# Twenty-seven pairs of blocks by seven products, with their sums of weight blocks made ahead in the up stage

## The chip, the core and the metric

The kernel runs on one core of a Trainium2 chip. The metric is device time in microseconds (us), the median of repeated runs. One more execution is recorded by the hardware profiler; its page and trace are read below. The engines are TensorE (PE, with its weight loads as PEld), VectorE (DVE), ScalarE (ACT), GpSimd (POOL) and SyncE (SP), which here mostly issues DMA transfers.

## The reference, cut to what matters

One layer of an encoder block over 256 tokens of width 2048, float32 throughout:

```python
hn = rmsnorm(h, mix_norm_pre);  proj = hn @ w_in            # then an SSD mixer and a pooling mixer
h = h + rmsnorm(concat([y_ssd, y_pool]) @ w_out, mix_norm_post)
hn = rmsnorm(h, ffn_norm_pre);  up = hn @ w_up              # 2048 x 11264: gate and value halves
ff = (gelu(dwconv(gate)) * val) @ w_down                    # 5632 x 2048
h = h + rmsnorm(ff, ffn_norm_post)
gate = sigmoid(rmsnorm(h, ple_norm_pre) @ w_ple_gate)       # 2048 x 2048
h = h + rmsnorm(gate * (p @ w_ple), ple_norm_post)
```

Nearly all work is in the products with the weight matrices, about 200 MB of float32 that are read from DRAM once.

## The kernel before

**Precision.** Each operand of a product is split into a high part (a ScalarE copy that rounds, L150) and a low part (a VectorE subtraction, L151). A product is three matmuls: high by high, high by low, low by high, all issued at L87 (`mm`).

**Stages.** In order: the input projections (`dtu`, `xb`, `z` in the trace, with the mixers among them), the output projection (`wo`), a small product (`ple`), **up** (`ga` for the gate half, `va` for the value half: 88 units of one 1 MB load and 32 matmuls each), **down** (`dn`), a second small product, and **gate** (`gt`). Down and gate each go through their output columns in two halves of 1024. A half of down is 22 pairs of 128-row blocks of the weight (u = 0 to 21), a half of gate is 8 pairs.

**A pair.** In `token_major` a regular pair loads 1 MB (two row blocks by 1024 columns) into one of three `raw` buffers, splits it into two of five `whi`/`wlo` buffers, and runs 24 matmuls of 128x512. The activations (`hs`) are split at L865 for each pair in down. In a *fast* pair the 2x2 blocks (two token blocks, two row blocks, two column blocks) are multiplied by seven products in place of eight, Winograd's form of Strassen's scheme: 21 matmuls (`seven_products`). It needs sums of the weight's four blocks, made by three VectorE additions in the raw buffer (L250 over 128x1024, L251 and L252 over 128x512), and sums of the activations' blocks (`pair_sums`, L753 to L758: four subtractions or additions over 128x128, and a split over 128x512). Its results gather in four more PSUM banks (`alt`; `dns`, `dn0s`, `dn1s`, `gts` in the trace), which `combine` adds into the main ones (L262 to L276) after the unit that follows the last fast pair of a half.

Fast pairs before: in `wo` u = 5 and u = 2, 4; in down `(2, 5, 8, 11, 14, 17)` and `(2, 5, 8, 11, 14, 17, 19)`; in gate u = 4 and u = 2. For the four row pairs that come first in down, `hid_sums` keeps the activations' sums in two pages (`hsum`), so that the second half has them ready.

**Memory.** There are 13 pages of 1 MB (128 x 2048 floats). During up and down, two hold h (the residual), six the hidden activations (`hid`), and others the normalised input, the `ple` product and what a stage gathers.

**Order.** The program is written as one stream; the Tile scheduler keeps that order on each engine, and adds semaphores. Loads of weights stand in order on SP's queue, so one that waits for a buffer holds up those behind it. Jobs in the list `work` are run by `aside()`, one entry after each unit. In the second half of down, before u = 16, `first_gate` loads the gate's first pair (`gtf`, 1 MB) into a page and splits it there: a ScalarE pass at L905, a second read of the weight with an accumulating GpSimd DMA, and a ScalarE copy at L907. At the end of down the residual is updated (L807) and transposed and split (`dnx`, L189) for the gate.

In the gate's second half the order of row blocks is permuted (`ks`), and pages that have come free (`spare`) take the parts of some pairs.

Of the kernel before, what the change touches and what calls it, by code (L numbers as in the profile page):

```python
# [11 lines left out]
F32 = mybir.dt.float32  # L12
F32R = mybir.dt.float32r
AF = mybir.ActivationFunctionType
ALU = mybir.AluOpType

P = 128
L = 256
D = 2048
NK = D // P  # L20
DSSD = 1024
H = 16
DFF = 5632
# [28 lines left out]
def build(nc, a, out):  # L52
    x = a["x"][0]
    w_in, w_out, w_up = a["w_in"][0], a["w_out"][0], a["w_ffn_up"][0]
    w_down, w_gate, w_ple = a["w_ffn_down"][0], a["w_ple_gate"][0], a["w_ple"][0]
    out = out[0]

    with tile.TileContext(nc) as tc, \
# [12 lines left out]
        def page(name, dtype=F32):  # L71
            return gp.tile([P, 2048], dtype, tag="pg", bufs=13, name=name)

        def mid(name, dtype=F32):
            return gp.tile([P, 1024], dtype, tag="mid", bufs=3, name=name)
# [38 lines left out]
        last, sums_ = {}, {}  # L114

        def load(dst, src, ahead=False):

            with tc.issue_after(last["dma"]) if last and not ahead else nullcontext():
                return ins(nc.sync.dma_start(dst, src))
# [72 lines left out]
        work = []  # L192
# [10 lines left out]
                yield o, c  # L203
                c += o.shape[-1]

        def block_sums(name, w, which):


            jobs = []

            def step(c0, k, i):
                t = sums_[name, c0, k]
                v = t.rearrange("p (b c) -> p b c", b=4)
                if i == 0:
                    nc.gpsimd.dma_start(t.rearrange("p (k c) -> p k c", k=2),
                                        w[k * P:(k + 2) * P, c0:c0 + 1024].rearrange("(k p) c -> p k c", p=P))
                elif i == 1:
                    nc.gpsimd.dma_start(v[:, 0:2], w[k * P:(k + 2) * P, c0 + 512:c0 + 1024]
                                        .rearrange("(k p) c -> p k c", p=P), accum_op=ALU.add)
                elif i == 2:  # L220
                    nc.gpsimd.dma_start(v[:, 3], v[:, 0], accum_op=ALU.add)
                else:
                    nc.gpsimd.dma_start(v[:, 2], v[:, 3], accum_op=ALU.add)

            for c0, k in which:
                sums_[name, c0, k] = dp.tile([P, 2048], F32, tag=f"{name}s{c0}_{k}", bufs=1, name=f"{name}s{c0}_{k}")
            for j in range(len(which) + 3):
                jobs.append([lambda a_=(*which[j - i], i): step(*a_) for i in (3, 2, 1, 0) if 0 <= j - i < len(which)])
            return jobs

        def seven_products(name, stage, w, k0, c0, a_, acc, alt, start, stop):

            if (stage, c0, k0) in sums_:
                r = raw(f"{name}r", None, 0, 0)
                last["dma"] = load(r[:, 512:1536], w[(k0 + 1) * P:(k0 + 2) * P, c0:c0 + 1024], True)
                last["dma"] = load(r[:, :512], w[k0 * P:(k0 + 1) * P, c0:c0 + 512], True)
                t = page(f"{name}t")
                last["dma"] = load(t, sums_[stage, c0, k0], True)  # L240
                b11 = split(f"{name}a", r[:, :512], 512)
                b2 = split(f"{name}b", r[:, 512:1536], 1024)
            else:
                r = t = raw(f"{name}r", w[k0 * P:(k0 + 2) * P, c0:c0 + 1024]
                            .rearrange("(k p) c -> p k c", p=P), 2, 1024)
                b11 = split(f"{name}a", r[:, :512], 512)
                b2 = split(f"{name}b", r[:, 1024:], 1024)
                v = r.rearrange("p (b c) -> p b c", b=4)

                nc.vector.tensor_add(v[:, 0:2], v[:, 0:2], v[:, 1::2])  # L250
                nc.vector.tensor_add(v[:, 3], v[:, 3], v[:, 0])  # L251
                nc.vector.tensor_add(v[:, 2], v[:, 2], v[:, 3])  # L252
            t13 = split(f"{name}c", t[:, :1024], 1024)
            t42 = split(f"{name}d", t[:, 1024:], 1024)
            for x, (wh, wl), c, o, own in (
                    ("a11", b11, 0, alt[0], True), ("a12", b2, 0, acc[0][0], False), ("s4", b2, 512, acc[0][1], False),
                    ("s1", t13, 0, alt[1], True), ("s3", t13, 512, alt[2], True), ("a22", t42, 0, acc[1][0], False),
                    ("s2", t42, 512, alt[3], True)):
                xh, xl = a_[x]
                for q, (xx, ww) in enumerate(((xh, wh), (xh, wl), (xl, wh))):  # L260
                    mm(o, xx, ww[:, c:c + 512], own and start and q == 0, own and stop and q == 2)
# [175 lines left out]
        for u in range(0, NK, 2):  # L437
            r = [wp.tile([P, 2048], F32, tag="raw", bufs=3, name=f"dtur{u}") if u else r0, page(f"dtur{u + 1}")]
            for j in range(2):
                k = u + j  # L440
# [17 lines left out]
            for j in range(2):  # L458
                k = u + j
# [373 lines left out]
        pl = [ple(0)]  # L833
        rf = row_rstd("rf", h)
        rfb = along_tokens("rfb", rf)
        hid = [page(f"hid{i}") for i in range(6)]
        for s in range(DFF // 512):
            sc = mid(f"gr{s}")
            for i in range(2):
                ga = main(f"ga{s}{i}")  # L840
                feature_pairs(f"ug{s}{i}", w_up, s * 512 + i * 256, hf, ga)
                o = sc[:, i * 512:(i + 1) * 512]
                total(o, ga)
                v = o.rearrange("p (f t) -> p f t", f=2)
                nc.vector.tensor_tensor(v, v, rfb.unsqueeze(1).to_broadcast([P, 2, L]), op=ALU.mult)
            cv = conv(f"fc{s}", sc, 3, V_FCW + 4 * s, NF, V_FCB + 4 * s)
            nc.scalar.activation(cv, cv, AF.Gelu_apprx_tanh)  # L847
            nc.gpsimd.tensor_tensor(cv.rearrange("p (f t) -> p f t", f=4), cv.rearrange("p (f t) -> p f t", f=4),  # L848
                                    rfb.unsqueeze(1).to_broadcast([P, 4, L]), op=ALU.mult)
            for i in range(2):  # L850
                va = main(f"va{s}{i}")
                feature_pairs(f"uv{s}{i}", w_up, DFF + s * 512 + i * 256, hf, va)
                c0 = (s % 2) * 1024 + i * 512
                hd = hid[s // 2][:, c0:c0 + 512]
                total(hd, va)
                nc.vector.tensor_mul(hd, hd, cv[:, i * 512:(i + 1) * 512])
# [3 lines left out]
        def get_hid(k):  # L860
            if k % 2 == 0:
                t = lp.tile([P, 1024], F32R, tag="hs", bufs=2, name=f"hs{k}")
                src = hid[k // 8][:, (k % 8) * L:(k % 8 + 2) * L]
                nc.scalar.copy(t[:, :512], src)
                nc.vector.tensor_sub(t[:, 512:], src, t[:, :512].bitcast(F32))  # L865
                cur["t"] = t
            o = (k % 2) * L
            return cur["t"][:, o:o + L], cur["t"][:, 512 + o:512 + o + L]
# [7 lines left out]
                hcache[k0], hcache[k0 + 1] = get_hid(k0), get_hid(k0 + 1)  # L876
            return hcache[k]

        keep, kept = [], {}

        def hid_sums(k):


            (h1, l1), (h2, l2) = get_hid(k), get_hid(k + 1)
            if k not in kept:
                src = hid[k // 8][:, (k % 8) * L:(k % 8 + 2) * L]
                a11, a21, a12, a22 = (src[:, i * P:(i + 1) * P] for i in range(4))
                n = len(kept)
                if n in (0, 2):
                    keep.append(page(f"hsum{k}", F32R))  # L890
                o = keep[-1][:, n % 2 * 1024:(n % 2 + 1) * 1024] if n < 4 else mid(f"he{k}", F32R)
                d = pair_sums(f"hd{k}", mid(f"hd{k}"), o, a11, a21, a12, a22)
                if n < 4:
                    kept[k] = d
            else:
                d = dict(kept[k])
            d.update(a11=(h1[:, :P], l1[:, :P]), a12=(h2[:, :P], l2[:, :P]), a22=(h2[:, P:], l2[:, P:]))
            return d

        def first_gate():  # L900

# [6 lines left out]
            for j in range(2):  # L908
                ready[f"gt00_{j}"] = hi[:, j * 1024:(j + 1) * 1024], lo[:, j * 1024:(j + 1) * 1024]

        hp = sublayer("dn", w_down, list(range(NF)), hid_get, gload("gffn", a["ffn_norm_post"][0]), h, V_PN,
                      fast=((2, 5, 8, 11, 14, 17), (2, 5, 8, 11, 14, 17, 19)), sums=hid_sums, at={16: first_gate})


        pl.append(ple(1))
# [33 lines left out]
        for half in range(2):  # L949
# [1 line left out]
            alt = [] if half else main(f"gts{half}")  # L951
            acc = [main(f"gt{half}{t}") for t in range(2)]
            alt += main(f"gts{half}") if half else []
            ks, fast = list(range(NK)), (4,)
            if half == 1:
                ks, fast = [0, 1, 2, 3, 8, 9, 4, 5, 6, 7, 10, 11, 12, 13, 14, 15], (2,)

                for i in (8, 10):
                    sh, sl = page(f"gth{i}", F32R), page(f"gtl{i}", F32R)
                    for j in range(2):  # L960
                        spare[f"gt1{ks[i]}_{j}"] = (sh[:, j * 1024:(j + 1) * 1024], sl[:, j * 1024:(j + 1) * 1024])
# [68 lines left out]
```

## Time and profile before

| what | before |
|---|---|
| median of 3 runs | 1143.8 us (1143.8 to 1144.74) |
| the profiled execution | 1143.09 us, of which the span is 1141.3 |
| granted TensorE clock | 0.997 |
| instructions in the span | 15449 |
| PE busy | 1122.0 us |
| DVE busy | 868.8 us |
| ACT busy | 611.0 us |
| DMA, mean over the span | 193 GB/s |
| read from and written to DRAM | 216.99 MB and 2.10 MB |
| stages: up, down, small product and gate | about 303–798, 798–1036, 1036–1132 us |

Times inside the trace count from the start of the span. "Busy" is the time in which an engine executes; the chain of waits is the path that ended last, followed back step by step. `x` with a number counts instructions.

### The profile page before, as it was taken

How to read it: one execution, taken by the hardware profiler on the slowest of the kernel's cores; microseconds unless marked ns; L12 is line 12 of the kernel's file. 1: busy time of each engine (PE TensorE's matmuls, PEld its weight loads, DVE VectorE, ACT ScalarE, POOL GpSimd, SP SyncE). 2: the span in 40 equal slices, each digit the busy share in tenths (PEclk: the TensorE clock that was granted, in tenths of full speed). 3: DMA queues.
4: the chain of work that ended last, by engine and by line, in shares of the span. 5: the costliest groups of instructions: out<-in, count | busy, mean ns of one | idle time of the engine just before them, and what ended most of it. 6: DMA issues, size and time to landing. Idle time of an engine off the chain costs nothing.

```text
span 1141.3 us, 15449 instructions
## 1 busy us (share of the span) xinstructions
PE 1122.0 (98%) x6018; PEld 966.0 (85%) x6018; DVE 868.8 (76%) x1140; ACT 611.0 (54%) x830; POOL 124.9 (11%) x124
## 2 busy tenths in 40 slices
PE   9998999999999999999999999999999999999996
PEld 9997987888888888888888888888888888778885
DVE  6579896699876666666766756668888888789895
ACT  6633543565674554444544544545555565656562
POOL 0274504200110000000000000000000000001001
PEclk9999999999999999999999999999999999999999
DMA  9952347555556555555555565556566656666552
GB/s 358 341 184 75 111 151 267 200 160 190 172 190 205 196 190 185 184 185 186 189 191 193 181 204 186 185 184 222 157 212 221 200 170 220 194 221 205 181 196 74
DMA packets 129866, 220.09 MB, mean 193 GB/s; under 512 B 3713, under 2 KB 96769, under 8 KB 128897
## 3 DMA queue, kind: packets, MB, share of 16 engines
q1 hardware_dynamic: 129232, 217.70, 57.4%
q0 software_dynamic: 272, 1.05, 0.5%
q8 instruction: 47, 0.77, 0.3%
q10 hardware_dynamic: 288, 0.36, 0.1%
q14 instruction: 27, 0.21, 0.1%
HBM read 216.99 MB, written 2.10 MB: 192 GB/s over the span
## 4 chain that ended last, share of the span: by engine, by line
PE 90%; DVE 6%; ACT 1%; DMA 1%; issue 1%; POOL 1%; DVEq 0%; POOLq 0%; ACTq 0%
PE va L87 22%; PE ga L87 21%; PE dna L87 15%; PE gt L87 7%; PE woa L87 7%; PE dtu L87 4%; PE z L87 4%; PE xbc L87 3%; DVE cv L422 2%; PE dns L87 1%; PE ple L87 1%; DMA dn134r<-w_ffn_down 1%; PE dn0s L87 1%; DVE w L635 1%; DVE xb_0l L151 1%
## 5 line engine op out<-in xcount | busy, mean ns | idle before, releaser
L87 PE MATMUL ga<-wox,ug_0h 128*128 128x512 f32 x352 | 125.5, 395 | 0.0
L87 PE MATMUL ga<-wox,ug_1h 128*128 128x512 f32 x352 | 125.1, 394 | 0.0
L87 PE MATMUL va<-wox,uv_1h 128*128 128x512 f32 x352 | 124.8, 393 | 0.0
L87 PE MATMUL va<-wox,uv_0h 128*128 128x512 f32 x352 | 124.8, 393 | 0.0
L87 PE MATMUL ga<-wox,ug_1l 128*128 128x256 f32 x352 | 99.1, 282 | 0.0
L87 PE MATMUL ga<-wox,ug_0l 128*128 128x256 f32 x352 | 99.1, 282 | 0.0
L87 PE MATMUL va<-wox,uv_1l 128*128 128x256 f32 x352 | 99.1, 281 | 0.0
L87 PE MATMUL va<-wox,uv_0l 128*128 128x256 f32 x352 | 99.1, 281 | 0.0
L87 PEld LDWEIGHTS va<-wox,uv_0h 128*128 128x128 f32 x352 | 66.1, 188 | 15.0
L87 PEld LDWEIGHTS va<-wox,uv_1h 128*128 128x128 f32 x352 | 66.1, 188 | 15.0
L87 PEld LDWEIGHTS ga<-wox,ug_0h 128*128 128x128 f32 x352 | 66.1, 188 | 14.9
L87 PEld LDWEIGHTS ga<-wox,ug_1h 128*128 128x128 f32 x352 | 66.1, 188 | 14.9
L87 PE MATMUL dna<-dn_0h,hs 128*128 128x512 f32 x248 | 76.2, 395 | 0.8 <-DVE hs L865 0.5
L87 PE MATMUL dna<-dn_1h,hs 128*128 128x512 f32 x248 | 75.7, 393 | 0.0
L848 POOL TENSOR_TENSOR fc<-fc,rfb 128x1024 f32<-128x1024 f32 x11 | 26.6, 2417 | 440.2 <-ACT fc L847 440.2
L87 PEld LDWEIGHTS ga<-wox,ug_0l 128*128 128x128 f32 x352 | 66.2, 188 | 0.1
L87 PEld LDWEIGHTS ga<-wox,ug_1l 128*128 128x128 f32 x352 | 66.2, 188 | 0.0
L87 PEld LDWEIGHTS va<-wox,uv_0l 128*128 128x128 f32 x352 | 66.2, 188 | 0.0
L87 PEld LDWEIGHTS va<-wox,uv_1l 128*128 128x128 f32 x352 | 66.2, 188 | 0.0
L87 PEld LDWEIGHTS dna<-dn_0h,hs 128*128 128x128 f32 x248 | 46.2, 188 | 13.1 <-DVE hs L865 2.5
L87 PEld LDWEIGHTS dna<-dn_1h,hs 128*128 128x128 f32 x248 | 46.5, 188 | 10.8
L87 PE MATMUL dna<-dn_0l,hs 128*128 128x512 f32 x124 | 40.2, 393 | 0.0
(1457 smaller groups left out, 2930.0 us busy)
## 6 DMA issues: line engine op xcount, KB each, us to landing
dn0r<-w_ffn_down SPq DMA_DIRECT2D x16, 1024.0 KB, 5.6
dn1r<-w_ffn_down SPq DMA_DIRECT2D x15, 1024.0 KB, 5.7
zr<-w_in SPq DMA_DIRECT2D x8, 1024.0 KB, 5.1
dtur<-w_in SPq DMA_DIRECT2D x14, 528.0 KB, 8.8
wo0r<-w_out SPq DMA_DIRECT2D x7, 1024.0 KB, 5.9
gt1r<-w_ple_gate SPq DMA_DIRECT2D x7, 1024.0 KB, 6.3
wo1r<-w_out SPq DMA_DIRECT2D x6, 1024.0 KB, 5.7
gt0r<-w_ple_gate SPq DMA_DIRECT2D x6, 1024.0 KB, 5.6
```

The source lines that it names most:

```text
L87: nc.tensor.matmul(o, lhsT, rhs, start=start, stop=stop, skip_group_check=True)
L151: last["dve"] = ins(nc.vector.tensor_sub(lo[:, s], src[:, s], hi[:, s].bitcast(F32)))
L422: nc.vector.scalar_tensor_tensor(o[:, lo:hi], i[:, lo + d:hi + d], vec(wcol + j * wstep + f), o[:, lo:hi], op0=ALU.mult, op1=ALU.add)
L635: nc.vector.scalar_tensor_tensor(w[:, h * P:(h + 1) * P], cbm[:, 0, g, t, :], dt[:, t, 8 * g + h:8 * g + h + 1], w[:, h * P:(h + 1) * P], ...
L848: nc.gpsimd.tensor_tensor(cv.rearrange("p (f t) -> p f t", f=4), cv.rearrange("p (f t) -> p f t", f=4), rfb.unsqueeze(1).to_broadcast([P, ...
```

## The change

- Down has 22 fast pairs, 11 in each half, and gate 5: u = 2, 4, 6 and u = 1, 2. The `wo` stage is as it was. The order of the gate's second half is permuted anew.
- The weight-block sums of these 27 pairs are made during up. For each, one 1 MB load on SP's queue fetches the two row blocks into a page, VectorE does the three additions there, and one 1 MB store on SP's queue writes the sums to DRAM. One such item belongs to three units of up, in the list `work`. The last two items (down, first half, row blocks 4 and 8) are not stored, their pages are kept.
- In a fast pair of down or gate the raw buffer takes 0.75 MB (the blocks used as they are, two loads), and a page takes the 1 MB of sums, loaded behind them on SP's queue, unless it was kept.
- h is stored to DRAM at the start of up and loaded into new pages before u = 13 of down's second half (`back`). The `hid` pages are taken one after the other as up fills them.
- `hid_sums` makes the activations' sums for all 22 fast pairs of down; none is kept.

```diff
+        def block_sums(name, w, c0, k, held):
+            pg = []
+            def fetch():
+                r = page(f"{name}b{c0}_{k}")
+                pg.append(r)
+                load(r.rearrange("p (k c) -> p k c", k=2),
+                     w[k * P:(k + 2) * P, c0:c0 + 1024].rearrange("(k p) c -> p k c", p=P))
+            def add():
+                add_blocks(pg[0])
+                if held:
+                    sums_[name, c0, k] = pg[0], True
+            def store():
+                if not held:
+                    t = dp.tile([P, 2048], F32, tag=f"{name}s{c0}_{k}", bufs=1, name=f"{name}s{c0}_{k}")
+                    load(t, pg[0])
+                    sums_[name, c0, k] = t, False
+            return [fetch], [], [add], [store]
+        def add_blocks(r):
+            v = r.rearrange("p (b c) -> p b c", b=4)
+            nc.vector.tensor_add(v[:, 0:2], v[:, 0:2], v[:, 1::2])
+            nc.vector.tensor_add(v[:, 3], v[:, 3], v[:, 0])
+            nc.vector.tensor_add(v[:, 2], v[:, 2], v[:, 3])
...
-                t = page(f"{name}t")
-                last["dma"] = load(t, sums_[stage, c0, k0], True)
+                t, held = sums_[stage, c0, k0]
+                if not held:
+                    t = page(f"{name}t")
+                    last["dma"] = load(t, sums_[stage, c0, k0][0], True)
...
-        hid = [page(f"hid{i}") for i in range(6)]
+        h_kept = []
+        for t in range(2):
+            h_kept.append(dp.tile([P, D], F32, tag=f"h{t}", bufs=1, name=f"h_kept{t}"))
+            load(h_kept[t], h[t])
+        dn_fast, gt_fast = ((2, 4, 6, 8, 9, 11, 13, 14, 16, 18, 19), (1, 3, 5, 7, 8, 10, 12, 14, 16, 17, 19)), ((2, 4, 6), (1, 2))
+        gt_ks = list(range(NK)), [0, 1, 4, 5, 8, 9, 2, 3, 6, 7, 10, 11, 12, 13, 14, 15]
+        which = [("dn", w_down, c * 1024, 2 * u) for c in range(2) for u in dn_fast[c]] + \
+            [("gt", w_gate, c * 1024, gt_ks[c][2 * u]) for c in range(2) for u in gt_fast[c]]
+        work.extend([] for _ in range(8 * DFF // 512))
+        for i, w_ in enumerate(which[2:] + which[:2]):
+            for j, jobs in enumerate(block_sums(*w_, i >= len(which) - 2)):
+                work[3 * i + 2 + j].extend(jobs)
+        hid = []
...
+                if len(hid) == s // 2:
+                    hid.append(page(f"hid{s // 2}"))
...
+        def back():
+            for t in range(2):
+                h[t] = page(f"hb{t}")
+                last["dma"] = load(h[t], h_kept[t])
...
-                      fast=((2, 5, 8, 11, 14, 17), (2, 5, 8, 11, 14, 17, 19)), sums=hid_sums, at={16: first_gate})
+                      fast=dn_fast, sums=hid_sums, at={13: back, 16: first_gate})
...
-            ks, fast = list(range(NK)), (4,)
+            ks, fast = gt_ks[half], gt_fast[half]
             if half == 1:
-                ks, fast = [0, 1, 2, 3, 8, 9, 4, 5, 6, 7, 10, 11, 12, 13, 14, 15], (2,)
```

More of the change, by code (lines that the diff above doesn't have):

```diff
@@ L204, in columns @@
                 c += o.shape[-1]
[L206 to L229, printed above, removed]
+        def block_sums(name, w, c0, k, held):
[20 more added lines that the diff above has]
+            nc.vector.tensor_add(v[:, 2], v[:, 2], v[:, 3])
         def seven_products(name, stage, w, k0, c0, a_, acc, alt, start, stop):
@@ L247, in seven_products @@
                 b2 = split(f"{name}b", r[:, 1024:], 1024)
[L248 to L252, printed above, removed]
+                add_blocks(r)
             t13 = split(f"{name}c", t[:, :1024], 1024)
@@ L877, in hid_get @@
             return hcache[k]
-        keep, kept = [], {}
         def hid_sums(k):
             (h1, l1), (h2, l2) = get_hid(k), get_hid(k + 1)
[L885 to L898, printed above, removed]
+            src = hid[k // 8][:, (k % 8) * L:(k % 8 + 2) * L]
+            d = pair_sums(f"hd{k}", mid(f"hd{k}"), mid(f"he{k}", F32R), *(src[:, i * P:(i + 1) * P] for i in range(4)))
+            return dict(d, a11=(h1[:, :P], l1[:, :P]), a12=(h2[:, :P], l2[:, :P]), a22=(h2[:, P:], l2[:, P:]))
+        def back():
+            for t in range(2):
+                h[t] = page(f"hb{t}")
+                last["dma"] = load(h[t], h_kept[t])
         def first_gate():
```

## The prediction

> **What bounds the kernel now.** The profile was read from the top: busy shares of the engines, the chain of waits, then tables by stage, then the vector engine's timeline within the stages that change. Shares of the span first, and the chain summed by engine:
>
> ```profile
> PE 1122.0 (98%) x6018; PEld 966.0 (85%) x6018; DVE 868.8 (76%) x1140; ACT 611.0 (54%) x830; POOL 124.9 (11%) x124
> PE 90%; DVE 6%; ACT 1%; DMA 1%; issue 1%; POOL 1%; DVEq 0%; POOLq 0%; ACTq 0%
> ```
>
> TensorE is the bound nearly everywhere, so a matmul taken out is worth its issue time unless something else becomes late. The chain in order of time (start, us, what) prices one matmul, and shows the only real stop of the down stage:
>
> ```profile
> 775.97 22.33 PE va L87 x128
> 798.30 11.11 PE dna L87 x48
> 809.40 0.69 PE dns L87 x3
> 810.09 1.38 PE dna L87 x6
> 811.47 0.69 PE dns L87 x3
> 814.22 11.11 PE dna L87 x48
> ...
> 979.85 11.12 PE dna L87 x48
> 991.05 1.24 DVE dn128dl L151
> 992.30 9.32 DMA dn134r<-w_ffn_down
> ```
>
> 48 matmuls of 512 columns take 11.11 us: 0.2315 each. A regular pair (24) is 5.55 us, a seven-product pair (21) 4.86, 0.694 less. Up runs without a gap, 22.33 per 128. At 991–1014 the chain leaves TensorE: a load, scalar and vector work are as late as the matmuls there. The table by stretch tells how near:
>
> ```profile
> core 0: us, PE busy (x) PEld busy (x) DVE busy (x) ACT busy (x) POOL busy (x), PEclk, DMA share, GB/s
> 303.00:798.00 495.00, 494.46 (x2843) 433.91 (x2842) 337.74 (x437) 256.76 (x347) 28.07 (x15) 1.00 0.58 189
> 798.00:912.00 114.00, 114.00 (x495) 92.64 (x494) 99.09 (x123) 66.35 (x82) 0.00 (x0) 1.00 0.61 195
> 912.00:1036.00 124.00, 122.54 (x526) 98.07 (x526) 105.43 (x123) 76.89 (x100) 3.97 (x7) 1.00 0.63 203
> 12.00:16.00 4.00, 4.00 (x27) 4.00 (x26) 3.66 (x7) 3.08 (x7) 0.00 (x0) 1.00 1.02 413
> 984.00:989.00 5.00, 5.00 (x24) 4.03 (x23) 4.20 (x5) 2.41 (x3) 0.00 (x0) 1.00 0.96 324
> ```
>
> Up (303–798) leaves the vector engine 157 us and the DMA engines 42% free. Down (798–1036) has VectorE at 86%, and PE idle for 1.46 us in its second half. DMA has moved 413 GB/s at 12–16 us, and 324 at 984–989 with its share at 0.96.
>
> **What is removed.** Down goes from 13 to 22 fast pairs, gate from 2 to 5. At three matmuls each that is 27 + 9 = 36 matmuls, 36 × 0.2315 = 8.3 us of PE (6.25 in down, 2.08 in gate). The sums of weight blocks also leave the vector engine in these stages:
>
> ```profile
> 832.96 1.23 DVE L250 TENSOR_TENSOR dn016r<-dn016r 128x1024 f32<-128x1024 f32 x1
> ...
> 835.36 0.69 DVE L251 TENSOR_TENSOR dn016r<-dn016r 128x512 f32<-128x512 f32 x1
> 836.09 0.69 DVE L252 TENSOR_TENSOR dn016r<-dn016r 128x512 f32<-128x512 f32 x1
> ```
>
> Back to back (starts 1.14 and 0.61 apart in this timeline) they cost 2.36 a pair.
>
> **Up: what is added.** 27 times 2.36 = 64 us of VectorE. In 495 us it goes from 338 to 402, 81%: work that fits beside the PE. One item belongs to three units of 5.58 us (22.33 / 4): for 25 items a 1 MB fetch and a 1 MB store, both on SP's queue among the three weight loads. SP's own issue, 0.37 us by its rows, is small against 5.58. But a store waits on SP for VectorE's third add, and behind it stand the next unit loads; the raw pool of three gives those loads a lead of about two units, 11 us, and the adds have one unit for their 2.36, so they should be done before SP comes to the store. Bytes: 3.17 MB of weights (189 GB/s × 16.75 us) plus 2.10 makes 5.27 MB in 16.75 us, 315 GB/s. That lies between rows that were reached (324 and 413, loads alone). No row has stores beside loads: before writes 2.10 MB in all. Bounds: 0 if the rate is held, as at 12–16; if only 300 were held, 17.57 − 16.75 = 0.82 us per item, about 20 us over 25 items. I take 0.4 us, for h's two stores and the first items at the ragged start of up (chain at 303–320): the row at 12–16 is nearest, for it too has 1 MB and half-MB loads queued back to back.
>
> The Trainium skill ("DMA: Bandwidth & Descriptors", section "Anatomy of one DMA") speaks against this part: a transfer's end is signalled only when the write is confirmed, which it says takes surprisingly long when the target is DRAM. No store here is read sooner than a stage later, apart from the held page that it frees, so by that rule the term would be a late page at most; the trace of before has no such store to weigh it against.
>
> **Down: what is added.** VectorE per pair, at the timeline's pitches: regular 2 × 1.14 + 0.60 = 2.88 (two 128x1024 splits at 1.14 and one hs at 0.60) under 5.55 of PE. Fast with sums made: 0.61 + 3 × 1.14 + 0.60 + hidden sums 1.4 (four 128x128 at 0.2, one 512 at 0.6) = 6.03 under 4.86; with adds in place it was 8.39. So 22 × 6.03 + 22 × 2.88 + about 12 for combines and tail = 208 us, against 204.5 measured in the two rows above, while PE falls from 236.5 to 230: VectorE at 90%. Dropping the kept hidden sums costs 4 × 1.4 of that. Fast–regular cycles need 8.91 in 10.41, fast–fast–regular (five of them: 8,9; 13,14; 18,19; 7,8; 16,17) 14.94 in 15.27. Locally a fast pair runs up a debt of 1.17 us, two 2.34, which the five whi/wlo buffers (two and a half regular units ahead) should carry. I cost it at nothing; without that cover it is 5 × 2.3 = 11.7 at most.
>
> Loads: a fast pair now moves 1.75 MB. Half 1: 11 × 1 + 11 × 1.75 + 2 for h coming back + 1 for the gate's first page = 33.25 MiB, 34.9 MB in 114.5 us, 305 GB/s; half 0, with two sums held in pages, about 260. Before, 203 GB/s with one late load cost 1.46 us. I take 0.6, bounds −1.4 (the old stop vanishes) and +3 (two such stops more, as the gate's page and h's two now stand among the loads).
>
> **Gate.** All times here on before's clock. The first fast pair moves from u=4 to u=2, which starts at 1056.4 and would end at 1061.3. VectorE's timeline is busy from 1038.0 to 1060.8 with 2.7 us of gaps, on the residual, sixteen x splits and weight splits; it now needs three pairs' x sums (0.69 + four of 0.28 each) up front and u=2's four splits. Laid out from 1053.6 in program order, the sums' low part ends near 1060.2, the third split near 1062.5, the fourth 1063.7; five matmuls (1.16) follow: end 1064.9, a stop of 3.5. The sums' page is the second bound: SP issues it after the load for u=5, which waits for a raw buffer freed by a split at 1053.6, so about 1054.2; a 1 MB load alone lands in 5.6 (gt0r row), behind another one in 8.5 to 9.3 (a load of h, dn134r). Landing at 1061.8 to 1063, with scalar 1.05 and vector 1.14 for each half of it, puts the end at 1066.5 to 1068.2: a stop of 5.2 to 6.9. I take 5.4: the load here stands behind another one. Kept range 3.5 to 6.9.
> Half turn: the combine of half 0 (four 512 adds and copies) now follows its last unit, beside the splits for half 1's fast u=1, u=2: 0.5 to 2, taken 0.8. The tail after the last matmul is unchanged.
>
> **Sum.** −8.3 + 0.4 + 0.6 + 5.4 + 0.8 = −1.1 on the profiled execution's 1143.1 (span 1141.3 and 1.8 around it): 1142.0. The median of runs, 1143.8, is 0.7 above that execution: 1142.7. About 0.2%, 2.3 us, is what a measurement of this kernel can tell from no change.
>
> **Rivals.** *Faster*: the gate's page lands in 5.6 and VectorE keeps ahead: stop 3.5 or less, nothing else lost: 1143.8 − 8.3 + 3.5 = 1139.0, at best 1135.5. For: PE was busy 100% of 798–912 in spite of the old adds. Against: the packed VectorE timeline at 1038–1061.
> *Slower, VectorE in down*: if the buffers do not carry a fast pair's 6.03, PE stops at every double. It decides once the second of a double finds its splits not done, more than 1.17 us late. Half of 11.7 lost: 1142.7 + 5.5 = 1148.2. For: hidden sums no longer kept, 98% in those cycles, and splits wait 1.0 us for ScalarE even before (dn016dl). Against: PE's full row 798–912, at 87% VectorE.
> *Slower, DMA in up*: from a held rate under 315 GB/s; at 300, +20: 1163. For: 281–324 near a share of one at 979–989; writes unproven. Against: 413 at 12–16.
> The Trainium skill (same page, "Measured") has 341 GB/s for a single 1 MB transfer, and above that for larger ones; by it up would just hold, as by the row at 12–16 us.
> That the change does not do what it says: the changed program, as built, has the 36 matmuls fewer on TensorE, so no chance is kept for it.
>
> **Chances.** Forecast 0.37, own range 1140.5 to 1145; faster rival 0.25 (1135.5 to 1140.5); VectorE 0.23 (1145 to 1152); DMA 0.12 (1150 to 1163); the rest 0.03, above. Under 1141.5: 0.25 + 0.08 of the forecast's = 0.33. From 1141.5 to 1146.1: 0.29 + 0.03 of the VectorE rival's = 0.32. Above: 0.35. The range 1137 to 1152 leaves out 0.08 below and 0.12 to 0.15 above.
>
> **What would show it.** Right: down some 6.2 shorter with PE idle under 2 us; up still 22.33 per 128; one stop of about 5 us in the gate's third unit, released by the low split of the sums' page; DMA in up near 315 GB/s. Wrong: gaps at the doubles released by VectorE; unit loads in up landing after their use; no stop in the gate.

## The result and the profile after

| | before | after |
|---|---|---|
| median of 19 runs each | 1144.15 us (1143.63 to 1145.74) | 1141.99 us (1140.2 to 1142.91) |
| profiled span | 1141.3 us | 1138.5 us |
| read from and written to DRAM | 216.99 and 2.10 MB | 266.54 and 30.41 MB |

The ratio is 0.9978, with a 95% interval of 0.9972 to 0.9984: faster by 2.2 us, where 1142.7 was forecast, 1.1 us under the 1143.8 known then. It lies at the edge of what was called no change. The small sum hides two large terms of opposite sign, a gain in down and a loss in the gate; the prediction had both, but both too small. The profiled execution of the changed kernel took 1140.26 us, 1.7 less than the median; its granted clock was 0.995, where 13 of the 19 executions had 0.992. So the two traces show 2.8 us of gain where the medians show 2.2, and what most executions lost in addition is not shown.

The busy shares and the chain by engine, on the page of the changed kernel:

```profile
PE 1115.9 (98%) x5982; PEld 962.5 (85%) x5982; DVE 935.8 (82%) x1277; ACT 637.6 (56%) x869; POOL 128.9 (11%) x124
PE 91%; DVE 5%; ACT 1%; DMA 1%; POOL 1%; issue 1%; DVEq 0%; POOLq 0%; ACTq 0%
```

There are 36 matmuls fewer, and VectorE is busier by 67 us: 57 of them in up (338 to 395, where 402 was forecast), 6 in down, 4 in the gate and after it. What bounds the kernel has not changed. The chain in order of time (start, us, what) shows where it still breaks:

```profile
775.88 22.33 PE va L87 x128
798.20 11.11 PE dna L87 x48
...
1022.95 4.15 PE dna L87 x18
1027.10 3.47 PE ple L87 x15
...
1045.02 8.06 DMA gt04t<-gts
1053.11 1.05 ACT gt04ch L150
1054.19 1.24 DVE gt04cl L151
1055.47 1.22 PE gts L87 x2
```

Up ends at 798.20, 0.1 us earlier than before. Down ends at 1027.10, where it was 1036.18. Then the chain leaves TensorE for the load of the gate's first page of sums. The table by stretch, with the same columns as before:

```profile
core 0: us, PE busy (x) PEld busy (x) DVE busy (x) ACT busy (x) POOL busy (x), PEclk, DMA share, GB/s
303.00:798.00 495.00, 494.45 (x2844) 434.62 (x2843) 395.19 (x507) 256.30 (x344) 29.48 (x15) 1.00 0.92 305
798.00:909.00 111.00, 111.00 (x483) 90.34 (x482) 99.89 (x140) 77.16 (x99) 0.00 (x0) 1.00 0.73 252
909.00:1030.00 121.00, 121.00 (x526) 98.39 (x525) 113.19 (x163) 88.84 (x119) 7.57 (x11) 1.00 0.88 307
1052.00:1054.00 2.00, 0.00 (x0) 0.00 (x0) 0.00 (x0) 0.89 (x1) 0.00 (x0) 1.00 1.03 434
1054.00:1056.00 2.00, 1.26 (x3) 0.80 (x4) 1.81 (x2) 2.00 (x4) 0.00 (x0) 0.75 1.00 422
1056.00:1058.00 2.00, 2.00 (x6) 1.55 (x5) 2.00 (x3) 1.94 (x4) 0.00 (x0) 0.50 0.47 197
1058.00:1060.00 2.00, 2.00 (x9) 1.61 (x9) 2.00 (x3) 1.20 (x2) 0.00 (x0) 0.90 0.08 16
```

Down has PE at 100%, up at 99.9% as before. At 1052–1054 PE does nothing while DMA runs at 434 GB/s. And when PE starts again, its granted clock is 0.75 and then 0.50 for a while: the stop costs more than its length. All waits of PE from the end of down on (engine, line, what it waited for, us in total, times, longest; `gt04` is the gate's first fast pair, `ch` and `cl` the high and low part of the first half of its page of sums):

```profile
PE gts L87 <- ACT gt04ch L150: 3.4, 1, 3.4
PE gt L87 <- ACT pl L822: 0.6, 1, 0.6
PE gts L87 <- DVE gt04cl L151: 0.5, 1, 0.5
PE gt L87 <- DVE gt14bl L151: 0.5, 1, 0.5
PE gt L87 <- ACT psp L761: 0.3, 1, 0.3
```

VectorE stood idle for most of the stop; its timeline has 2.69 us of idle, ended by the high part of the page:

```profile
1054.19 1.23 DVE L151 TENSOR_TENSOR gt04cl<-gt04t,gt04ch 128x1024 fp32r<-128x1024 f32 x1 [2.69 <-ACT gt04ch L150]
```

**Where the 2.8 us of span come from.** Start of down −0.1. Down took 237.88 us (798.30 to 1036.18) and takes 228.90: −8.98. The gate, first to last matmul, took 89.92 (1042.54 to 1132.46) and takes 96.00 (1033.37 to 1129.37): +6.08. The small product between them −0.09, what follows the last matmul +0.29. Together −2.80.

### The profile page after: what moved, and what is told of

The parts are those of the page before. It is cut to its first block, busy times and chain, and to the rows that moved or that the text cites. A ratio compares the mean times of both kernels' runs of the same rounds, so it can differ in the third digit from the quotient of the medians.

```text
span 1138.5 us, 15770 instructions
## 1 busy us (share of the span) xinstructions
PE 1115.9 (98%) x5982; PEld 962.5 (85%) x5982; DVE 935.8 (82%) x1277; ACT 637.6 (56%) x869; POOL 128.9 (11%) x124
## 3 DMA queue, kind: packets, MB, share of 16 engines
HBM read 266.54 MB, written 30.41 MB: 261 GB/s over the span
## 4 chain that ended last, share of the span: by engine, by line
PE 91%; DVE 5%; ACT 1%; DMA 1%; POOL 1%; issue 1%; DVEq 0%; POOLq 0%; ACTq 0%
PE va L87 22%; PE ga L87 21%; PE dna L87 15%; PE woa L87 7%; PE gt L87 4%; PE dtu L87 4%; PE z L87 4%; PE xbc L87 3%; PE dns L87 3%; DVE cv L426 2%; PE dn0s L87 1%; PE dn1s L87 1%; PE ple L87 1%; DMA gt04t<-gts 1%; DVE w L639 1%
## 5 line engine op out<-in xcount | busy, mean ns | idle before, releaser
L87 PE MATMUL dna<-dn_0h,hs 128*128 128x512 f32 x176 | 54.8, 394 | 0.0
L87 PE MATMUL dna<-dn_1h,hs 128*128 128x512 f32 x176 | 54.6, 393 | 0.0
L233 DVE TENSOR_TENSOR dnb<-dnb 128x1024 f32<-128x1024 f32 x22 | 28.0, 1271 | 16.1 <-DMA dnb<-w_ffn_down 16.1
L87 PEld LDWEIGHTS dna<-dn_1h,hs 128*128 128x128 f32 x176 | 33.1, 188 | 7.7
L87 PEld LDWEIGHTS dna<-dn_0h,hs 128*128 128x128 f32 x176 | 33.0, 188 | 7.6
## 6 DMA issues: line engine op xcount, KB each, us to landing
dnb<-w_ffn_down SPq DMA_DIRECT2D x22, 1024.0 KB, 10.2
```

Of the source, the lines that this page charges most:

```text
L87: nc.tensor.matmul(o, lhsT, rhs, start=start, stop=stop, skip_group_check=True)
```

## The experiments

Two theories were set against each other for the gate. Theory 1: its first fast pair waits for a late page, and this, not the pairs' work or VectorE, eats the gain. The rival: VectorE is so packed there, or all loads so late, that any arrangement stalls. Further runs asked what the work in up buys, how near its limit up is, and why down gained 2.7 us more than its matmuls. Each is compared with runs of the kernel before on the same chip. The edits are shortened to the lines that matter, and comments are added to them.

**1. The gate as before** (22 pairs in down kept)

```diff
-gt_fast = ((2, 4, 6), (1, 2))
+gt_fast = ((4,), (2,))          # sums added in the raw buffer, old order of row blocks
```

> Down with its 22 pairs and the sums made in up as in the changed kernel; the gate stage as it was before (u = 4 and u = 2, sums added in the raw buffer, the old order of row blocks). Theory 1 (the gate's own change costs more than it brings: its first fast pair waits for its page of sums, then runs at half clock): down stays at 229.1 us without a gap, the gate's stretch falls from 96.0 us back to about 89.9, so 6.1 us less than the changed kernel: span about 1132.4, median about 1135.9. Rival (the gate is late because down ends sooner, so that its loads, h and the x splits come too late whatever its pairs are): 3 us or more of the stop stay, median 1139 or above.

Measured 1135.06 us, ratio 0.9920 (0.9907 to 0.9934). PE waits nowhere between 330 and 1130 us. Down is as fast as in the changed kernel, and the gate's change costs some 7 us of median: theory 1 in kind, at slightly more than its size (6.1 was forecast, from the trace).

**2. The first half's fast pairs at u = 4 and 6**

```diff
-gt_fast = ((2, 4, 6), (1, 2))
+gt_fast = ((4, 6), (1, 2))
```

> As the changed kernel, but the gate's first half has its fast pairs at u = 4 and 6, not at 2, 4 and 6. Theory 1: the sums' page of u = 4 is issued no later than now and has two more units (11 us), so the stop of 6.0 us and most of the 1.4 us of small waits ahead of it go; one pair less gives back 0.7: 5 to 6.5 us under the changed kernel, median 1135.5 to 1137. Rival (VectorE in the gate is the bound: three pairs' sums and splits): the stop moves to u = 4 and 3 us or more of it stay, median 1139 or above.

Measured 1135.95 us, ratio 0.9932 (0.9919 to 0.9944). The one wait that is left is at the turn of the gate's halves:

```profile
PE gts L87 <- DVE gt14al L151: 1.2, 1, 1.2
```

So the stop belonged to the pair at u = 2, and does not follow to u = 4. The combine at the turn costs 1.2 us of wait (0.8 was forecast).

**3. The page of the gate's first fast pair is kept from up on**

```diff
-        for i, w_ in enumerate(which[2:] + which[:2]):
-            for j, jobs in enumerate(block_sums(*w_, i >= len(which) - 2)):
+        g0 = which.index(("gt", w_gate, 0, 4))
+        for i, w_ in enumerate(which[:g0] + which[g0 + 1:] + which[g0:g0 + 1]):
+            for j, jobs in enumerate(block_sums(*w_, i >= len(which) - 1)):
```

> As the changed kernel, but the page that is kept from up on is that of the gate's first fast pair, and down's first two pages of sums are stored and loaded like the others. Theory 1 (the page's landing at 1053.1 is what the third unit waits for): with the page at hand its splits follow the x sums, VectorE's 2.7 us of idle at 1051.5 to 1054.2 are used, the wait for gt04ch (3.4 us) goes and with it the half clock of 3.4 us: 4 to 5.5 us under the changed kernel, median 1136.5 to 1138. Rival (VectorE and ScalarE are so packed there that the splits come no earlier than the page did): under 2 us gained, median 1140 or above. Down could lose up to 2 us at its start, where two pages more are loaded.

Measured 1135.27 us, ratio 0.9924 (0.9912 to 0.9937), 6.7 us under the changed kernel, more than forecast. The same five pairs, and of the five waits the two on the page are gone; the other three stay as they were:

```profile
PE gt L87 <- ACT pl L822: 0.6, 1, 0.6
PE gt L87 <- DVE gt14bl L151: 0.5, 1, 0.5
PE gt L87 <- ACT psp L761: 0.3, 1, 0.3
```

The stretches that held the stop, in this kernel:

```profile
1052.00:1054.00 2.00, 2.00 (x10) 1.65 (x9) 2.00 (x3) 2.00 (x5) 0.00 (x0) 1.00 0.30 127
1054.00:1056.00 2.00, 2.00 (x10) 1.61 (x9) 2.00 (x4) 1.96 (x3) 0.00 (x0) 1.00 0.11 18
1056.00:1058.00 2.00, 2.00 (x11) 1.60 (x10) 2.00 (x2) 1.05 (x1) 0.00 (x0) 1.00 0.95 285
```

PE full, clock 1.00. The late page was the cause both of the stop and of the slow clock behind it, and VectorE had the time. But the result only equals run 1, which has three pairs fewer in the gate: those pairs' 2.08 us go into the three small waits (1.4 us by this table, 2.1 by the starts of the matmuls around them in the changed kernel, where the second matmul after such a wait starts 0.34 us behind the first and not 0.23).

**4. Sums of the first fast pair in the raw buffer**

```diff
+which.remove(("gt", w_gate, 0, 4))      # this pair needs no page; its three adds run in the gate
```

> As the changed kernel, but the gate's first fast pair (first half, u = 2) makes its sums in the raw buffer, so that it needs no page; the other 26 keep theirs from up. Theory 1 (the late page alone makes the stop of 6.0 us): VectorE has 2.7 us of idle at 1051.5 to 1054.2 and now 2.36 us of adds more: the stop shrinks to 1 to 2.5 us and the half clock after it goes, 3.5 to 5 us under the changed kernel: 1137 to 1138.5. Rival (VectorE's floor of 3.5 us that was forecast): under 2.5 us gained, median 1139.5 or above.

Measured 1141.84 us, ratio 0.9980 (0.9971 to 0.9989): the time that the rival gave, and not for its reason. The stop at u = 2 is gone, with 0.2 us left where 3.4 were, in spite of 2.36 us more of VectorE. It has come back later:

```profile
PE gt L87 <- DVE gt_1l L151: 2.9, 1, 2.9
PE gts L87 <- ACT gt012ch L150: 1.0, 1, 1.0
```

The adds hold the raw buffer longer, so that a regular pair's load is issued at 1053.74 and the page of the third fast pair only at 1064.39 (8.3 us to landing), where the changed kernel issued it at 1049.08. A stop of 2.9 us at 1085–1090 follows, again with a lowered clock (0.66 in 1090–1095), and the chain leads back from it through VectorE's work to the landing of that page. The floor of VectorE that the prediction named is refuted by the trace, though the time alone would have spoken for it. The split that PE waits for comes at 1088.62, behind the first half's closing work (vg); what ordered it so was not followed up.

**5. Down's sums made during down**

```diff
-        which = [("dn", w_down, c * 1024, 2 * u) for c in range(2) for u in dn_fast[c]] + \
-            [("gt", w_gate, c * 1024, gt_ks[c][2 * u]) for c in range(2) for u in gt_fast[c]]
+        which = [("gt", w_gate, c * 1024, gt_ks[c][2 * u]) for c in range(2) for u in gt_fast[c]]
...
-        for i, w_ in enumerate(which[2:] + which[:2]):
-            for j, jobs in enumerate(block_sums(*w_, i >= len(which) - 2)):
+        for i, w_ in enumerate(which):
+            for j, jobs in enumerate(block_sums(*w_, False)):
```

> As the changed kernel, but the sums of down's 22 pairs are added in the raw buffer during down; only the gate's five are made in up. Theory 1 (VectorE would be down's bound without the work in up): 22 x 8.39 + 22 x 2.88 + 12 = 260 us of VectorE against 229 of TensorE: down about 260, median about 1173. Rival (down was never near VectorE's limit, as PE showed no gap before at 87%; the buffers carry it): under 10 us longer, median under 1152.

Measured 1187.18 us (one run). Down's stretch, 798.28 to 1073.97:

```profile
798.28:1073.97 275.69, 251.05 (x993) 188.72 (x993) 260.56 (x365) 164.79 (x215) 5.10 (x6) 0.96 0.56 179
```

VectorE's 260.6 us are the 260 that were counted, but the stretch is 15 us longer than that, 46.8 over the changed kernel's 228.90. The forecast took VectorE's work alone; PE's waits there name ScalarE's high parts more often than VectorE's low ones, and the clock is 0.96. Without the work in up, 22 pairs are far slower than 13: that is what the items for down buy.

**6. An item of sums for every two units of up**

```diff
-work[3 * i + 2 + j].extend(jobs)
+work[2 * i + 2 + j].extend(jobs)
```

> As the changed kernel, but an item of sums (1 MB fetched, 1 MB stored) belongs to two units of up, not three, so that all are done after 56 of 88 units: 4.2 MB in 11.16 us, 376 GB/s. Theory 1 (up is close to what the DMA engines can carry, 0.92 of their time at 305 GB/s): they give at most 330 or so, each item takes about 1.5 us more than its two units, and up grows by 20 to 40 us. Rival (there is room, as at 434 GB/s beside the gate's late page): up stays at 495 us, and the median within 1 us of 1142.

Measured 1162.76 us (one run); down starts at 820.21, 22.0 us later. A table of it:

```profile
330.00:620.00 290.00, 274.66 (x1546) 235.42 (x1545) 231.83 (x295) 130.60 (x177) 16.95 (x6) 1.00 0.99 348
641.00:798.00 157.00, 157.00 (x902) 137.81 (x901) 104.00 (x132) 78.15 (x104) 7.20 (x3) 1.00 0.60 197
```

While items are in flight DMA has no time left (0.99) and moves 348 GB/s, the most this mix of loads and stores reached; 376 were asked for. VectorE (232 of 290) is no busier than in the changed kernel, which has 235 in the same stretch, at 319 GB/s and a share of 0.96. So the rival of a DMA bound in up was close by: DMA time is used up at about 348 GB/s, and the changed kernel lies 8% below that rate. It is not shown that DMA alone set the pace. ScalarE's first part of a unit waits for unit loads in this stretch, but PE's longest waits end with a low part of VectorE:

```profile
PE ga L87 <- DVE ug_0l L151: 13.2, 11, 1.6
```

In the chain at 401–406 and 413–419 that part stands behind additions of an item (dnb). Items with the additions elsewhere, at the same rate of transfers, would tell the two apart; that was not run.

**7. The kernel before, with the gate's first page one pair earlier**

```diff
-at={16: first_gate}
+at={15: first_gate}
```

> The kernel before, with only the gate's first page (gtf and its second, accumulating read) moved one pair earlier, from u = 16 to u = 15 of down's second half. Down lost 1.46 us of PE idle there, and down's stretch shortened by 2.7 us more than its matmuls explain. Theory 1 (the stop at 1008 to 1032 comes from the transfer for the fast pair u = 17, which starts as late as its raw buffer comes free and runs beside the accumulating read, 9.3 us): a regular pair now meets that read, the stop goes, 1.5 to 2.8 us faster, median 1141.2 to 1142.5. Rival (VectorE with its sums in place at u = 14, 17 and 19 is the cause): no change, within 0.5 us of 1144.0.

Measured 1140.96 us, ratio 0.9971 (0.9959 to 0.9983): 3.0 us for one number, and more than the whole change brought. PE no longer waits anywhere in down. The load that had ended last (dn134r) is issued at 991.0, not 992.3, and lands after 7.8 us, not 9.3. So the kernel before had a loss of its own in down, and the changed kernel is rid of it by luck: nothing in the change was meant for it, and which part of the change removed it was not tested.

**8. 25 and 23 pairs in down, with the old gate**

```diff
-dn_fast = (2, 4, 6, 8, 9, 11, ...), (1, 3, 5, 7, 8, ...)                       # 11 and 11
+dn_fast = (2, 4, 6, 7, 9, 10, 12, 13, 15, 16, 18, 19), (1, 2, 4, 5, 7, 8, 10, 11, 13, 14, 16, 17, 19)   # 25
+dn_fast = (2, 4, 5, 7, 8, 10, 11, 13, 14, 16, 17, 19), (1, 3, 5, 7, 8, 10, 12, 14, 16, 17, 19)          # 23
```

> As the run with the old gate, but with 25 fast pairs in down, 12 and 13, nearly all in the pattern fast, fast, regular: VectorE 25 x 6.03 + 19 x 2.88 + 12 = 217.5 us for 227 of TensorE, and in the second half about 322 GB/s. Theory 1 (the five buffers carry the doubles; VectorE isn't yet the bound at 14.94 in 15.27): 9 matmuls less, -2.1 us against that run's 1135.06: 1133.0. Rival (at the doubles VectorE or the loads stop PE, 0.5 to 1 us at each): no gain or 2 to 6 us slower, 1135 to 1141, with waits of PE for low splits in down.

> As the run with the old gate, but down's first half has 12 fast pairs, mostly fast, fast, regular; the second half keeps its 11. Theory 1 (what 25 pairs lost was lost at the turn of the halves and in the second half, at 316 GB/s and with fast pairs at u = 1 and 2): no stop in the first half (257 GB/s, VectorE at 90%), 3 matmuls less: -0.7 against 1135.06, 1134.4. Rival (five buffers do not carry so many doubles in a row): 1135 to 1138 with waits for low splits in the first half.

Measured 1138.42 us (1135.71 to 1139.58), ratio 0.9945 (0.9932 to 0.9958), and 1134.64 us, ratio 0.9919 (0.9906 to 0.9933). One more pair in the first half costs nothing and brings 0.4 of its 0.7, less than these runs can tell. Three more, two of them in the second half, lose 3.4. The profiled execution of 25 took 1135.71 us, 2.7 less than the median, and shows waits of only 0.2 us in down, with the page for u = 1 landing 8.0 us after its issue and 0.7 us of wait in the gate. What the other four lost is not shown; the rival's size is right, its place is open. The 23-pair kernel has the lowest median of all that ran, 0.4 us under run 1, and beats both given kernels.

**9. Other arrangements of the gate**

```diff
-gt_fast = ((2, 4, 6), (1, 2))
+gt_fast = ((4,), (1, 2))         # the one
+gt_fast = ((2, 4), (2,))         # the other, with the page kept as in run 3 and the old order of row blocks
```

> As the changed kernel, but the gate's fast pairs are u = 4 in the first half and u = 1, 2 in the second, with the sums from up. Theory 1 (what is lost in the gate is lost where a fast pair stands early, at the first half's u = 2, or next to the other half's combine): the combine of the first half now comes two units before its end, PE has no gap in the gate, three matmuls less than with the old gate: -0.7 against 1135.06, 1134.4. Rival (in the second half the two pairs u = 1, 2 stall at the turn whatever the combine does, 1.2 us as with u = 4 and 6): 1135 to 1136.

> As the run with the gate's page held, but the gate's fast pairs are u = 2 and 4 in the first half, u = 2 in the second, with the old order of row blocks. Theory 1 (a pair more than the old gate, with the combine away from the turn): 0.7 less than 1135.06 by the matmuls, about 0.9 given back to the two small waits ahead of u = 2 that the run with the held page still shows: 1135.0 to 1135.5. Rival (those waits belong to the pairs that are now gone): 1134.4.

Measured 1135.47 us, ratio 0.9923 (0.9909 to 0.9937), and 1135.93 us, ratio 0.9931 (0.9917 to 0.9945). In the first PE waits only 0.2 us in the gate, so the stall at the turn that the rival named did not come, and yet the time is the rival's and not the 1134.4 of theory 1; why is open. In the second the two small waits ahead of u = 2 stay (0.6 and 0.3), and one of 1.0 us in down is new. Neither beats the old gate: within the noise of these runs, three to five fast pairs there are worth what two are.

## Why the prediction was right

The time, 1141.99, lies 0.7 under the forecast, inside its own range. Term by term, against the two traces:

| step | forecast | measured |
|---|---|---|
| 36 matmuls | −8.3 | −8.3 |
| up: sums, DMA, queue | +0.4 | −0.1 |
| down beside the matmuls | +0.6 (−1.4 to +3) | −2.7 (−8.98 + 6.25) |
| small product | 0 | −0.1 |
| gate, first fast pair | +5.4 (3.5 to 6.9) | +6.0, and 1.4 of waits ahead of it |
| gate, turn of the halves | +0.8 | +0.7 |
| tail | 0 | +0.3 |
| sum | −1.1 | −2.8 |

That the sum came within 0.7 us of the median is partly luck. In the trace, down was forecast 3.3 us too long and up 0.5, while the gate was forecast 1.9 us too short; the errors of opposite sign cancel.

**The step that failed is down's.** The old stop was priced at its 1.46 us of PE idle, and thought to survive in another form, with −1.4 as the most that could be won. It vanished, and was worth 2.7, outside those bounds. The stretches from 798.00 to the end of down, before and after:

```profile
798.00:1036.18 238.18, 236.72 (x1021) 190.86 (x1020) 204.70 (x245) 143.42 (x181) 4.05 (x8) 1.00 0.62 199
798.00:1027.10 229.10, 229.10 (x994) 186.40 (x993) 210.56 (x299) 164.51 (x215) 4.94 (x8) 1.00 0.81 280
```

Beside the 1.46 of idle, PE's busy time fell by 7.6 us; 27 matmuls are 6.25 of it, and 0.1 is up's earlier end. The other 1.3 us had counted as busy, and show in the times at which matmuls start. In down of the kernel before they start 0.231 us apart on average, except at five places from 996.8 to 1031.8, of which PE's list of waits names two. One of the five, with the time of each start first:

```profile
1010.55 0.39 PE L87 MATMUL dna<-dn134dh,hs 128*128 128x512 f32 x1
1011.62 0.50 PE L87 MATMUL dna<-dn134dl,hs 128*128 128x512 f32 x1 [0.69 <-DVE dn134dl L151]
1011.96 0.39 PE L87 MATMUL dna<-dn134dh,hs 128*128 128x512 f32 x1
```

From the first start to the second are 1.07 us, 0.84 more than usual, though the idle is 0.69; the next start is 0.34 behind. Over the five places the late starts add up to 2.8 us. In down of the changed kernel no two starts are more than 0.26 apart. Run 7 shows the size from the other side, 3.0 us with nothing else changed. Runs 1 and 7, both without such a loss and with the old gate, differ by 5.9 us, against 6.25 for down's 27 matmuls: what the seven products themselves bring in down.

**The gate's step held in its mechanism**, and the layout by hand of the late page held. The page was to be issued at 1054.2 and to land at 1061.8 to 1063 on before's clock, which is 9.1 us ahead at that point: 1045.1, and 1052.7 to 1053.9. It was issued at 1045.0 and landed at 1053.1; with the load ahead of it (1044.55) and a further page behind it (1045.49) it was one of three transfers of 1 MB issued within 1 us. PE was released by the page's high part and then, for 0.5 us more, by its low part, where the prediction named the low part alone. The start-to-start gap of the matmuls is 3.6 us over the normal one there, 0.7 at the next wait, and 1.6 more go to the lowered clock. The other bound given, VectorE's 3.5 us floor, was wrong: runs 3 and 4 leave 0.2 us or less of it. It was laid out with that pair's weight splits behind the x sums, while in the trace two of them (gt04al, gt04bl) were done by 1044.5, among the x splits. The lowered clock was not in the sum; that 5.4 is close to 6.0 is luck to that extent, since the stop itself was 4.3 us by the starts. Nor were the 1.4 us ahead of the pair in any term.

**The rivals.** VectorE in down was wrong at 22 pairs: the five doubles carried, PE full, VectorE at 92% (213 of 232 us in the two stretches). With the adds in place (run 5) its 260.6 us are the largest part of a stretch of 275.7. (Half of the 11.7 us in that rival is 5.9, not 5.5; nothing else rests on it.) DMA in up did not decide at 319 GB/s (315 was forecast); with 376 asked for (run 6) its time was used up, and up grew by 22 us. The faster rival, 1139.0, described the gate without a late page; runs 2 and 3 show that this alone would have given 1135 to 1136, since the old stop in down was gone too.

**The rule on stores.** The stores of sums landed 8.3 us (gts) and 7.3 us (those of down) after their issue, by the medians; the fetches for them, on the same queue in the same stage, took 9.5 and 10.2. They were read stages later, and no wait of PE or of SP's queue names one. The Trainium skill ("DMA: Bandwidth & Descriptors", "Anatomy of one DMA") tells, of transfers issued from GpSimd, of late completion when DRAM is the target; these stores, issued from SP, cost no wait by it.

## What to carry to other kernels

Price a removed instruction at its issue time, and then look for what stood still beside it, from start to start and not by idle time: here an old loss was worth twice its idle, and a one-line move of a load brought more than the large change. Work moved ahead, into a stage with idle engines, comes back as a transfer; here that transfer was late at its first use after a change of stage, where no buffer came free early. Keep that one in its page, and leave the optimisation out where few units would use it.

## What the runs showed of the hardware

After a PE stop of 3.4 us the granted clock went to half for 3.4 us (0.75, 0.50 and 0.90 in the three stretches of 2 us), which cost 1.6 us more; after the 2.9 us stop of run 4 it fell as well (0.66 in 1090–1095). In run 2, whose longest stop is 1.2 us, and in up of run 6, through repeated stops of up to 1.6 us, it stayed at 1.00. In run 5 it fell behind stops that were no longer, 1.1 us at 847.6 and 1.5 us at 879.4, each with shorter waits close by:

```profile
846.00:850.00 4.00, 2.40 (x10) 1.23 (x8) 4.00 (x6) 1.05 (x1) 0.00 (x0) 1.00 0.63 223
850.00:854.00 4.00, 4.00 (x10) 2.50 (x11) 3.73 (x8) 3.43 (x4) 0.00 (x0) 0.57 0.01 2
876.00:880.00 4.00, 3.27 (x14) 2.02 (x12) 3.83 (x6) 1.32 (x3) 0.00 (x0) 1.00 0.74 241
880.00:884.00 4.00, 2.94 (x6) 1.65 (x7) 3.73 (x9) 2.05 (x3) 0.00 (x0) 0.63 0.05 22
```

So the length of one stop does not decide; what does is not shown. The Trainium skill ("TensorE: Matmul & The Clock Gate", "Part 1: The HAM clock gate") tells of a window of about 3.4 us and a half rate after an idle window. The 3.4 us of half clock agree; that it takes an idle window is not borne out by the stops of 2.9, 1.5 and 1.1 us.

Loads and stores together reached 348 GB/s at a DMA share of 0.99, as a mean over 290 us in run 6; loads alone ran at 434 over 2 us in the changed kernel (1052–1054). That the stores make the difference is not shown.
